# Two heads at a time in a prompt's attention, zero-padded score and latent operands, and another order at two joints

## The chip, the cores and the metric

The kernel runs on one core of one Trainium2 chip. The time is the device time of one execution in microseconds; of several runs the median is quoted. The engines are TensorE (PE in the profile, its weight loads PEld), VectorE (DVE), ScalarE (ACT), GpSimd (POOL) and SyncE (SP), which issues most transfers.

## The reference

Two layers of an encoder trunk run over 640 rows of 1024 channels: one prompt of 512 rows and eight streams of 16 new rows, each stream with 512 rows of past. A layer projects x to the inputs of three mixers and their gates, runs the mixers, merges them, and runs a squared-ReLU feed-forward, each of the two with a layer norm behind it. The mixer that matters here is latent attention with eight heads:

```
q_lat = einsum('bqhd,chd->bqhc', q_nope, w_uk)
s = einsum('bqhc,bkc->bhqk', q_lat, ckv) + einsum('bqhr,bkr->bhqk', q_rope, krope)
s = where(k_pos // 64 <= q_pos // 64, s * scale, -1e30)
p = softmax(s)
o_lat = einsum('bhqk,bkc->bqhc', p, ckv)
out = einsum('bqhc,chd->bqhd', o_lat, w_uv)
```

A head has 64 plain and 32 rotary dimensions, the latent has 256, values have 64. All is fp32.

## The kernel before, in words

Activations lie with channels on the partitions and the 640 rows along the free axis, in two halves of 320 (index i of names such as `x`, `r`, `P`). Most products are made exact to fp32 by three products in a rounded format: an operand is cut into a high and a low part (helper `split`, L378 on ScalarE and L379 on VectorE), and `mm3_steps` issues high x high (L437), low x high (L439) and high x low (L441). Other products are plain fp32 matmuls; the profile has two records for one of them, and one for a transpose. An order listing has one row for each instruction.

The prompt's attention is not absorbed: for each head `keys` and `queries` make 96-row operands, 64 plain rows and 32 rotary ones, cut in two (`kth`, `ktl`, `qh`, `ql`; three buffers of each). `heads_in(pr)` makes them for a pair of heads. The stage has 32 steps in a layer, one for each head h and block of 128 queries qt, in the order h = i // 4, qt = i % 4. Step i issues `score(i + 2)` (128 x up to 512 keys, three products), `value(i - 1)`, one piece of other work, `turn_p(i)` (transposes of the weights, tile `tp`, evicted to `pT`) and two more pieces. The softmax of a score goes over VectorE (mask, maximum), ScalarE (exponential with its sum) and VectorE (reciprocal, scaling). `value` multiplies into a tile `op` that holds a pair of heads: the even head in partitions 0 to 63, the odd one in 64 to 127. The pieces of other work are `heads_in` of the next pair, side projections (`mm_ca`, `mm_cg`, `mm_gc`, `mm_h`, three products each), and in the last eight steps `absorb`, which makes the streams' latent queries: `qlat` multiplies 64 rows of a head's `w_uk` by 64 rows of `qsn`, the streams' plain queries.

Behind it the streams run absorbed: `cut_keys(b)` cuts a stream's keys (`kT`, and for four streams together the rotary rows `kR`) into `kTh`, `kTl`, `kRh`, `kRl`; `rope_q(g)` lays the rotary queries of four streams into a tile with zeros elsewhere (`qzh`, `qzl`), and `score_s` (tile `ss`) multiplies three blocks, two of `kT` and one of `kR`, with three products each. Later `uv` turns the latent outputs into values, for two heads at a time.

Before the feed-forward stands a layer norm whose second half of rows is done under the first products of the first half: `plain(f, i)` makes the hidden block f for half i in 24 matmuls (tile `P`); `norm_starts` sums columns with ones (`pvn`), VectorE iterates the root (`rsyn`), `spread` broadcasts it (`rbn`), and `norm_cut` makes r and the cut x (`xh` on ScalarE, `xl` on VectorE, eight blocks). The first block of the second half needs all eight.

TensorE's instructions stand in the order in which the code issues them. On the other engines a scheduler sets the order by priorities; `first` raises that of the attention's own work, and `issue_after` holds an instruction behind a named one.

## Time and profile before

| | |
|---|---|
| median of 3 runs | 1978.42 us (1977.46 to 1981.24) |
| the profiled execution, its own time | 1979.2 us |
| its span | 1977.4 us |
| TensorE busy | 1953.8 us, 99% of the span |
| VectorE, ScalarE, GpSimd busy | 1349.3, 949.8 and 24.7 us |
| chain of work that ended last | 96% TensorE, 2% ScalarE, 1% VectorE |

The profile's times are those of the span, which begins with the first instruction and ends with the last; 1.8 us of the execution lie outside of it. A row of the timeline gives the start, the duration, engine, line, operation, output and inputs with partitions x elements, how many of them in a row, and in brackets the idle time ahead and what ended it. Matmuls overlap: a matmul's duration is longer than the time until the next may start, so the distance from start to start is what one costs. The line numbers are those of the kernel before.

### The profile page before, as it was taken

To read this page: it belongs to the slowest core of one execution; us is meant where nothing else is said; L and a number is where in the kernel's file an instruction comes from. 1 tells how busy PE (TensorE), PEld (TensorE's weight loads), DVE (VectorE), ACT (ScalarE), POOL (GpSimd) and SP (SyncE) were. 2 spreads that over 40 slices of the span, in tenths; PEclk is the share of its full clock that TensorE was granted. 3 is DMA by queue.
4 is the path that set the end of the run, shared out by engine and by line. 5 is a ranking of instruction groups with operands and counts; after the bars stand their busy time and mean duration, and the time that the engine had idled before them with its cause. 6 is when DMAs were issued, how large, how long until landed. Compare 5 with 4: busy or idle time off the path is not lost.

```text
span 1977.4 us, 33150 instructions
## 1 busy us (share of the span) xinstructions
PE 1953.8 (99%) x13264; PEld 1898.1 (96%) x13264; DVE 1349.3 (68%) x2936; ACT 949.8 (48%) x1880; POOL 24.7 (1%) x55
## 2 busy tenths in 40 slices
PE   9999999999999999999999999999999999999997
PEld 9887999999999999999997879999999999999997
DVE  5765669776586666776777556797755866667675
ACT  5564322244475545446556643323354665553473
POOL 0000000000000000000000000000000000000000
PEclk9999999999999999999999999999999999999998
DMA  6112322222222333213341134222232133332242
GB/s 204 52 36 92 131 81 82 77 66 85 65 75 83 121 128 118 86 65 107 108 155 57 36 96 148 66 82 65 75 90 62 58 107 122 114 107 86 64 129 75
DMA packets 59691, 180.62 MB, mean 91 GB/s; under 512 B 10384, under 2 KB 12832, under 8 KB 59536
## 3 DMA queue, kind: packets, MB, share of 16 engines
q1 hardware_dynamic: 57472, 172.01, 27.2%
q0 software_dynamic: 2064, 6.48, 1.1%
q8 instruction: 104, 1.70, 0.4%
q14 instruction: 51, 0.42, 0.1%
HBM read 173.78 MB, written 4.69 MB: 90 GB/s over the span
## 4 chain that ended last, share of the span: by engine, by line
PE 96%; ACT 2%; DVE 1%; DMA 0%; issue 0%; ACTq 0%; DVEq 0%
PE f L441 8%; PE f L439 8%; PE f L437 8%; PE mm_g L437 6%; PE mm_g L441 6%; PE mm_g L439 6%; PE op L817 2%; PE mix L437 2%; PE mix L439 2%; PE mix L441 2%; PE B L441 2%; PE C L437 2%; PE B L439 2%; PE C L441 2%; PE A L437 2%; PE C L439 2%
## 5 line engine op out<-in xcount | busy, mean ns | idle before, releaser
L226 ACT ACTIVATE wh<-raw 128x1024 fp32r<-128x1024 f32 (+3 forms) x170 | 166.7, 981 | 306.1 <-PE mm_g L439 201.2
L227 DVE TENSOR_TENSOR wl<-raw,wh 128x1024 fp32r<-128x1024 f32 (+3 forms) x170 | 191.4, 1126 | 129.6 <-ACT wh L226 126.2
L439 PE MATMUL f<-hl,wh 128*128 128x320 f32 x992 | 252.0, 309 | 0.0
L441 PE MATMUL f<-hh,wl 128*128 128x320 f32 x992 | 251.7, 309 | 0.0
L437 PE MATMUL f<-hh,wh 128*128 128x320 f32 x992 | 249.5, 309 | 0.0
L437 PE MATMUL mm_g<-xh,wh 128*128 128x320 f32 x768 | 181.9, 311 | 0.0
L441 PE MATMUL mm_g<-xh,wl 128*128 128x320 f32 x768 | 181.1, 309 | 0.0
L439 PE MATMUL mm_g<-xl,wh 128*128 128x320 f32 x768 | 180.4, 309 | 0.0
L439 PEld LDWEIGHTS f<-hl,wh 128*128 128x128 f32 x992 | 172.5, 188 | 0.0
L441 PEld LDWEIGHTS f<-hh,wl 128*128 128x128 f32 x992 | 172.3, 188 | 0.0
L437 PEld LDWEIGHTS f<-hh,wh 128*128 128x128 f32 x992 | 171.9, 188 | 0.0
L1077 DVE SCALAR_TENSOR_TENSOR cv<-U,vec,cv 128x320 f32<-128x320 f32 x360 | 134.4, 436 | 0.0
L437 PEld LDWEIGHTS mm_g<-xh,wh 128*128 128x128 f32 x768 | 129.8, 188 | 1.5 <-issue 0.3
L441 PEld LDWEIGHTS mm_g<-xh,wl 128*128 128x128 f32 x768 | 129.6, 188 | 0.2
L439 PEld LDWEIGHTS mm_g<-xl,wh 128*128 128x128 f32 x768 | 129.4, 188 | 0.0
L412 DVE TENSOR_TENSOR r<-r,f 128x320 f32<-128x320 f32 x192 | 85.4, 483 | 55.0 <-PE f L441 54.4
L226 ACT ACTIVATE wh<-sm 128x1024 fp32r<-128x1024 f32 x56 | 59.4, 1060 | 121.2 <-DVE sm L261 44.7
L227 DVE TENSOR_TENSOR wl<-sm,wh 128x1024 fp32r<-128x1024 f32 x56 | 68.5, 1223 | 49.9 <-PE C L441 28.6
L437 PE MATMUL mix<-mgh,wh 128*128 128x320 f32 x256 | 79.4, 311 | 0.0
L439 PE MATMUL mix<-mgl,wh 128*128 128x320 f32 x256 | 78.7, 309 | 0.0
L441 PE MATMUL mix<-mgh,wl 128*128 128x320 f32 x256 | 75.2, 309 | 0.0
L226 ACT ACTIVATE wh<-rx 128x1024 fp32r<-128x1024 f32 x28 | 29.7, 1060 | 89.2 <-PE f L439 76.9
(438 smaller groups left out, 5135.7 us busy)
## 6 DMA issues: line engine op xcount, KB each, us to landing
raw<-in_W_dram SPq DMA_DIRECT2D x204, 512.0 KB, 3.6
rx<-in_W_dram SPq DMA_DIRECT2D x28, 512.0 KB, 3.7
rxb<-in_W_dram SPq DMA_DIRECT2D x28, 512.0 KB, 3.7
kT<-in_ckvT_dram SPq DMA_DIRECT2D x16, 512.0 KB, 4.2
kM<-in_ckvM_dram SPq DMA_DIRECT2D x16, 512.0 KB, 4.0
raw<-in_W_dram SPq DMA_DIRECT2D x18, 384.0 KB, 3.1
raw<-in_W_dram SPq DMA_DIRECT2D x12, 256.0 KB, 2.7
x<-in_xT_dram SPq DMA_DIRECT2D x8, 320.0 KB, 6.1
```

Of the source, the lines that this page charges most:

```text
L226: nc.scalar.activation(out=wh[:, :n], in_=src, func=AF.Copy)
L227: nc.vector.tensor_tensor(out=wl[:, :n], in0=src, in1=R(wh[:, :n]), op=ALU.subtract)
L412: nc.vector.tensor_tensor(out=r[i][:, m, :], in0=r[i][:, m, :], in1=o, op=ALU.add)
L437: nc.tensor.matmul(o, wh, h[k], start=st, stop=False, skip_group_check=more)
L439: nc.tensor.matmul(o, wh, lo[k], start=False, stop=False, skip_group_check=more)
L441: nc.tensor.matmul(o, wl, h[k], start=False, stop=sp, skip_group_check=more)
L817: nc.tensor.matmul(op[r0:r0 + 64, qt * P:(qt + 1) * P], vt[kt // 2][:, kt % 2, h * 64:(h + 1) * 64], pT[:, kt * P:(kt + 1) * P], start=kt ...
L1077: nc.vector.scalar_tensor_tensor(out=o, in0=u, scalar=tap, in1=o, op0=ALU.mult, op1=ALU.add)
```

## The change

In the prompt's attention the steps now go through a pair of heads in the order of `PAIR`, both heads in turn. `value` does nothing for the even head and, with the odd one, issues the matmuls of both alternately, into the two column halves of the array. Key and query operands become 128-row tiles, three of each, whose rows 96 to 127 GpSimd fills with zeros once a layer. `qsn` gets 128 rows for every head, zeros in the half that belongs to the other head, and `qlat` multiplies all 128 rows. One gated tile buffer goes. `cut_keys` cuts the plain keys ahead of the rotary ones, and `rope_q` of the first streams is issued behind them. In the feed-forward, `pvn` and `rbn` are issued in the middle of a block's 24 matmuls, where they stood between blocks. The computed values are the same sums; the two layers are changed alike.

```diff
SIDE = (("ca", 0), ("cg", 0), ("ca", 1), ("cg", 1), ("gc", 0), ("h", 0), ("gc", 1), ("h", 1), ("gb", 0), ("gb", 1))
+PAIR = ((0, 0), (0, 1), (1, 0), (0, 2), (1, 1), (0, 3), (1, 2), (1, 3))
 KT2 = 2 * KT
...
     nc.vector.memset(one1, 1.0)
+    zero = cst.tile([P, 1], F32, name="zero")
+    nc.vector.memset(zero, 0.0)
     wu = psT.tile([P, 512], F32, tag="t", name="wu")
...
         qnl = pq.tile([P, 3, T], F32R, tag="qn", name="qnl", bufs=2)
-        qsn = pq.tile([P, 4, P], F32, tag="qsn", name="qsn", bufs=1)
+        qsn = pq.tile([P, 2, 4, P], F32, tag="qsn", name="qsn", bufs=1)
+        nc.gpsimd.memset(qsn, 0.0)
         vt = [pq.tile([P, 2, 512], F32, tag="kM", name=f"vt{i}", bufs=2) for i in range(2)]
...
             if n != "h" and n != "gb":
-                t = held[n] = pf.tile([P, T], F32, tag="g2" if n == "cg" else "g1", name=f"{n}s{l}{c}", bufs=1 if n == "cg" else 2)
+                t = held[n] = pf.tile([P, T], F32, tag="g2" if n == "cg" else "g1", name=f"{n}s{l}{c}", bufs=1)
             for i, a, b in HALVES:
...
         pp = pp_stk.enter_context(pool(f"pp{l}", side="right"))
-        kth = [pp.tile([96, SEQ], F32R, name=f"kth{i}") for i in range(3)]
-        ktl = [pp.tile([96, SEQ], F32R, name=f"ktl{i}") for i in range(3)]
+        kth, ktl, qth, qtl = ([pp.tile([P, SEQ], F32R, name=f"{n}{i}") for i in range(3)] for n in ("kth", "ktl", "qth", "qtl"))
+        for i in range(3):
+            for t in (kth[i], qth[i], ktl[i], qtl[i]):
+                nc.gpsimd.tensor_copy(t[96:P, :], zero[96:P, 0:1].to_broadcast([32, SEQ]))
         def key_rope(i):
...
             for e in range(2):
-                qk.append((pp.tile([96, SEQ], F32R, tag="qh", name=f"qh{l}_{pr}_{e}", bufs=3), pp.tile([96, SEQ], F32R, tag="ql", name=f"ql{l}_{pr}_{e}", bufs=3)))
+                qk.append((qth[(2 * pr + e) % 3], qtl[(2 * pr + e) % 3]))
             @first
             def queries(i, c0, c1, o):
...
                 if i:
-                    nc.scalar.activation(out=qsn[:, pr, :], in_=o[:, SEQ - HF:], func=AF.Copy, scale=SCALE)
+                    for e in range(2):
+                        nc.scalar.activation(out=qsn[64 * e:64 * e + 64, e, pr, :], in_=o[64 * e:64 * e + 64, SEQ - HF:], func=AF.Copy, scale=SCALE)
             @first
             def keys(ko):
...
                 yield
+        def at_step(i):
+            e, qt = PAIR[i % 8]
+            return 2 * (i // 8) + e, qt
         @first
         def score(i):
-            h, qt = divmod(i, 4)
+            h, qt = at_step(i)
             qh, ql, kh, kl = qt_h[h]
...
         def turn_p(i):
-            h, qt = divmod(i, 4)
+            h, qt = at_step(i)
             n, pb = P * (qt + 1), mid.pop(i)
...
             nc.scalar.activation(out=pT[:, :n], in_=tp[:, :n], func=AF.Copy)
-            pv[i] = pT
+            pv[h, qt] = pT
         @first
         def value(i):
-            h, qt = divmod(i, 4)
-            pT, pr, r0 = pv.pop(i), h // 2, 64 * (h % 2)
-            if i % 8 == 0:
+            h, qt = at_step(i)
+            if h % 2 == 0:
+                return
+            pr = h // 2
+            if qt == 0:
                 pv["o"] = mm_tile(f"op{l}_{pr}", 512, "op")
             op = pv["o"]
+            pTs = [pv.pop((2 * pr + e, qt)) for e in range(2)]
             for kt in range(qt + 1):
-                nc.tensor.matmul(op[r0:r0 + 64, qt * P:(qt + 1) * P], vt[kt // 2][:, kt % 2, h * 64:(h + 1) * 64], pT[:, kt * P:(kt + 1) * P], start=kt == 0, stop=kt == qt)
-            if i % 8 == 7 and pr < 3:
+                for e in range(2):
+                    hd = 2 * pr + e
+                    nc.tensor.matmul(op[64 * e:64 * e + 64, qt * P:(qt + 1) * P], vt[kt // 2][:, kt % 2, hd * 64:(hd + 1) * 64], pTs[e][:, kt * P:(kt + 1) * P], start=kt == 0, stop=kt == qt)
+            if qt == 3 and pr < 3:
                 nc.scalar.activation(out=oT[:, pr, :SEQ], in_=op, func=AF.Copy)
...
             for ct in range(2):
-                os = [mm_tile(f"qlat{l}{ct}{e}", 512) for e in range(2)]
-                for pr in range(4):
-                    for e, o in enumerate(os):
-                        nc.tensor.matmul(o[:, pr * P:(pr + 1) * P], wukT[64 * e:64 * e + 64, pr, ct * P:(ct + 1) * P], qsn[64 * e:64 * e + 64, pr, :], start=True, stop=True)
+                for e in range(2):
+                    o = mm_tile(f"qlat{l}{ct}{e}", 512)
+                    for pr in range(4):
+                        nc.tensor.matmul(o[:, pr * P:(pr + 1) * P], wukT[:, pr, ct * P:(ct + 1) * P], qsn[:, e, pr, :], start=True, stop=True)
                         if pr == 3:
...
             def cut_keys(b):
...
                 kt_s[b] = [ps.tile([P, 2, NK], F32R, tag=f"kT{n}", name=f"kT{n}{l}{b}", bufs=2) for n in "hl"]
+                nc.vector.tensor_copy(kT[:, :, PAST:], ckv[:, :, SEQ + b * NQ:SEQ + (b + 1) * NQ])
+                ins = split(*kt_s[b], kT)
                 if kR is not None:
...
                         nc.vector.tensor_copy(kR[rg, PAST:], krope[rg, SEQ + (b + j) * NQ:SEQ + (b + j + 1) * NQ])
-                nc.vector.tensor_copy(kT[:, :, PAST:], ckv[:, :, SEQ + b * NQ:SEQ + (b + 1) * NQ])
-                ins = split(*kt_s[b], kT)
-                if kR is not None:
                     split(*kr_s[b // 4], kR)
...
                 nc.gpsimd.memset(t, 0.0)
-            for z in qz:
-                nc.scalar.activation(out=z, in_=cnew.rearrange("p b (j q) -> p (b j) q", j=2), func=AF.Copy)
-            @first
-            def rope_q(g):
-                for j in range(4):
-                    rg = slice(DR * j, DR * j + DR)
-                    split(qz[0][rg, j, :], qz[1][rg, j, :], qsr[rg, g].rearrange("p h q -> p (h q)"))
+            def rope_q(g, after=(None, None)):
+                for n in range(2):
+                    with tc.issue_after(after[n].ins) if after[n] else ExitStack():
+                        if g == 0:
+                            nc.scalar.activation(out=qz[n], in_=cnew.rearrange("p b (j q) -> p (b j) q", j=2), func=AF.Copy)
+                        for j in range(4):
+                            rg = slice(DR * j, DR * j + DR)
+                            src, dh = qsr[rg, g].rearrange("p h q -> p (h q)"), qz[0][rg, j, :]
+                            if n == 0:
+                                nc.scalar.activation(out=dh, in_=src, func=AF.Copy)
+                            else:
+                                nc.vector.tensor_tensor(out=qz[1][rg, j, :], in0=src, in1=R(dh), op=ALU.subtract)
             olat = pq.tile([P, 2, NH, NB, NQ], F32, tag="qr", name=f"olat{l}", bufs=1)
...
                 nc.scalar.activation(out=oT[:, 3, :SEQ], in_=pv["o"], func=AF.Copy)
-            rope_q(0)
+            first(rope_q)(0, (i_h, i_l))
             with tc.issue_after(i_l.ins):
...
                     cut_keys(4)
-                    rope_q(1)
+                    first(rope_q)(1)
                 if b % 2 and b < NB - 1:
...
             x_blk = {}
-            def plain(f, i):
+            def plain(f, i, between=None):
                 if i == 0:
                     x_blk[f] = W.next(l, ("ff1", 0, f), hold=True)
-                o = bank(f"P{l}_{f}_{i}")
-                prod(o, [x_blk[f]("ff1", k, f) for k in range(KT)], xs_of((i,))[0])
+                o, ret = bank(f"P{l}_{f}_{i}"), None
+                for k, _ in enumerate(mm3_steps([o], [x_blk[f]("ff1", k, f) for k in range(KT)], xs_of((i,)))):
+                    if k == 3 and between:
+                        ret = between()
                 if i:
...
                 hidden(f, i, work(f"h{f}_{i}"), o)
+                return ret
             X = chunk(7)
             plain(X[0], 0)
-            spread = ahead(norm_starts, 1, ss1[1], ntp)
-            plain(X[1], 0)
-            rb1 = ahead(spread)
+            spread = plain(X[1], 0, lambda: ahead(norm_starts, 1, ss1[1], ntp))
+            rb1 = plain(X[2], 0, lambda: ahead(spread))
             ahead(norm_cut, 1, rb1)
-            plain(X[2], 0)
             plain(X[3], 0)
```

TensorE, layer 0, the first values of the first pair of heads (tile `op`; around them scores `s`, a side projection `mm_ca`, the next pair's queries `uqn` and transposes `tp`). Before:

```order
L437 MATMUL s_0_3_1075<-kth_909,qh_0_0_939 128x512
L439 MATMUL s_0_3_1075<-ktl_912,qh_0_0_939 128x512
L441 MATMUL s_0_3_1075<-kth_909,ql_0_0_940 128x512
L817 MATMUL op_0_1086<-pT_0_0_1065,vt_209 64x128
L437 MATMUL mm_ca_1_1_1071<-xh_100,wh_842 128x320
L439 MATMUL mm_ca_1_1_1071<-xl_102,wh_842 128x320
L441 MATMUL mm_ca_1_1_1071<-xh_100,wl_843 128x320
L804 MATMUL tp_0_1_1091<-ident,p_0_1_1039 128x128 x2
```

and after:

```order
L441 MATMUL s_0_3_1153<-kth_912,qth_918 128x512
L443 MATMUL s_0_3_1153<-ktl_915,qth_918 128x512
L445 MATMUL s_0_3_1153<-kth_912,qtl_921 128x512
L837 MATMUL op_0_1164<-pT_0_0_1083,vt_212 64x128
L837 MATMUL op_0_1164<-pT_1_0_1141,vt_212 64x128
L441 MATMUL uqn_1_1_1167<-qnh,wh_954 128x320
L443 MATMUL uqn_1_1_1167<-qnl,wh_954 128x320
L445 MATMUL uqn_1_1_1167<-qnh,wl_955 128x320
L818 MATMUL tp_0_2_1171<-ident,p_0_2_1100 128x128 x3
```

The value matmul of head 1's first block (`pT_1_0`) has moved up to head 0's; in longer groups the two heads alternate for two, three and four blocks in the same way.

TensorE, layer 0, a step of the last pair, with the two `qlat` of the step (their operands are `qsn` and the weights `wukT`). Before:

```order
L437 MATMUL s_6_3_1858<-kth_909,qh_3_0_1645 128x512
L439 MATMUL s_6_3_1858<-ktl_912,qh_3_0_1645 128x512
L441 MATMUL s_6_3_1858<-kth_909,ql_3_0_1646 128x512
L817 MATMUL op_3_1869<-pT_6_0_1852,vt_209 64x128
L835 MATMUL qlat_1847<-qsn,wukT_1761 128x128
L804 MATMUL tp_6_1_1872<-ident,p_6_1_1799 128x128 x2
L835 MATMUL qlat_1848<-qsn,wukT_1761 128x128
L437 MATMUL mm_h_0_0_1812<-xh_99,wh_1527 128x320
```

and after:

```order
L441 MATMUL s_6_3_1910<-kth_912,qth_918 128x512
L443 MATMUL s_6_3_1910<-ktl_915,qth_918 128x512
L445 MATMUL s_6_3_1910<-kth_912,qtl_921 128x512
L837 MATMUL op_3_1921<-pT_6_0_1860,vt_212 64x128
L837 MATMUL op_3_1921<-pT_7_0_1904,vt_212 64x128
L854 MATMUL qlat_1900<-qsn,wukT_1765 128x128
L818 MATMUL tp_6_2_1925<-ident,p_6_2_1873 128x128 x3
L854 MATMUL qlat_1900<-qsn,wukT_1765 128x128
L441 MATMUL mm_h_0_0_1817<-xh_101,wh_1532 128x320
```

The two `qlat` of a step still stand on both sides of the transposes, but now belong to one head and one output tile, and half of the steps have no values.

VectorE, layer 0, behind the broadcast root of the second half's norm (`t` are pieces of a combination for a later stage, `hl` and `T1l` low parts of hidden blocks and of that combination). Before:

```order
L1168 SCALAR_TENSOR_TENSOR r_4551<-r_4551,vec,rbn_6024 128x320 x8
L1182 TENSOR_TENSOR t_00_6119<-r_4551,r_4550 128x320
L379 TENSOR_TENSOR hl_15_0_6019<-h_00_6017,hh_15_0_6018 128x320
L1182 TENSOR_TENSOR t_01_6123<-r_4551,r_4550 128x320
L1152 SCALAR_TENSOR_TENSOR xl_102<-r_4551,vec,xh_100 128x320
L1182 TENSOR_TENSOR t_02_6127<-r_4551,r_4550 128x320
L1152 SCALAR_TENSOR_TENSOR xl_102<-r_4551,vec,xh_100 128x320
L1182 TENSOR_TENSOR t_03_6131<-r_4551,r_4550 128x320
L1152 SCALAR_TENSOR_TENSOR xl_102<-r_4551,vec,xh_100 128x320 x4
L1186 SCALAR_TENSOR_TENSOR t_00_6135<-r_4551,vec,t_00_6119 128x320
L1152 SCALAR_TENSOR_TENSOR xl_102<-r_4551,vec,xh_100 128x320 x2
```

and after, from the first `xl` on:

```order
L1175 SCALAR_TENSOR_TENSOR xl_104<-r_4560,vec,xh_102 128x320
L1205 TENSOR_TENSOR t_02_6136<-r_4560,r_4559 128x320
L1175 SCALAR_TENSOR_TENSOR xl_104<-r_4560,vec,xh_102 128x320
L1205 TENSOR_TENSOR t_03_6140<-r_4560,r_4559 128x320
L1175 SCALAR_TENSOR_TENSOR xl_104<-r_4560,vec,xh_102 128x320 x3
L1209 SCALAR_TENSOR_TENSOR t_00_6144<-r_4560,vec,t_00_6128 128x320
L1175 SCALAR_TENSOR_TENSOR xl_104<-r_4560,vec,xh_102 128x320
L1209 SCALAR_TENSOR_TENSOR t_01_6148<-r_4560,vec,t_01_6132 128x320
L1175 SCALAR_TENSOR_TENSOR xl_104<-r_4560,vec,xh_102 128x320
L383 TENSOR_TENSOR hl_30_0_6064<-h_00_6062,hh_30_0_6063 128x320
L1209 SCALAR_TENSOR_TENSOR t_02_6152<-r_4560,vec,t_02_6136 128x320
L1175 SCALAR_TENSOR_TENSOR xl_104<-r_4560,vec,xh_102 128x320
```

Two more combination pieces and a low part of another hidden block have moved ahead of the last `xl`.

## Rows read from the trace of the kernel before

**Rows 1.** The page's busy times: us, share of the span, instructions.

```profile
PE 1953.8 (99%) x13264; PEld 1898.1 (96%) x13264; DVE 1349.3 (68%) x2936; ACT 949.8 (48%) x1880; POOL 24.7 (1%) x55
```

**Rows 2.** TensorE's waits: who waited for whom, us, times, longest.

```profile
PE ss L439 <- DVE kTl L379: 5.0, 2, 2.5
...
PE pvn L462 <- DVE s L417: 2.4, 2, 1.4
```

**Rows 3.** Stretches of layer 0's attention: busy us of each engine, clock, DMA.

```profile
123.40:147.60 24.20, 24.20 (x153) 19.89 (x152) 15.13 (x44) 15.28 (x39) 1.45 (x2) 1.00 0.11 28
160.00:186.50 26.50, 26.50 (x156) 19.77 (x155) 11.33 (x35) 13.17 (x33) 0.84 (x3) 1.00 0.16 52
```

**Rows 4.** TensorE's timeline around two groups of values: start, us, operation.

```profile
92.50 0.28 PE L439 MATMUL s<-ktl,qh 96*128 96x256 f32 x1
92.62 0.28 PE L441 MATMUL s<-kth,ql 96*128 96x256 f32 x1
92.83 0.65 PE L817 MATMUL op<-pT,vt 128*64 128x128 f32 x4
93.41 0.41 PE L437 MATMUL uqn<-qnh,wh 128*128 128x320 f32 x1
93.66 0.31 PE L439 MATMUL uqn<-qnl,wh 128*128 128x320 f32 x1
93.81 0.31 PE L441 MATMUL uqn<-qnh,wl 128*128 128x320 f32 x1
...
95.62 0.87 PE L817 MATMUL op<-pT,vt 128*64 128x128 f32 x6
```

**Rows 5.** TensorE's timeline at the streams' value projection in layer 0.

```profile
269.84 1.97 PE L1024 MATMUL uv<-olat,wuv 128*64 128x128 f32 x32
271.74 0.41 PE L437 MATMUL mm_g<-xh,wh 128*128 128x320 f32 x1
```

**Rows 6.** Groups of instructions by line and shape: count, busy us, mean ns, idle before.

```profile
L817 PE MATMUL op<-pT,vt 128*64 128x128 f32 x320 | 48.6, 283 | 0.0
```

**Rows 7.** TensorE's timeline in a step with latent queries, layer 0.

```profile
165.40 0.28 PE L441 MATMUL s<-kth,ql 96*128 96x256 f32 x1
...
166.19 0.49 PE L835 MATMUL qlat<-qsn,wukT 64*128 64x128 f32 x2
166.61 0.55 PE L804 MATMUL tp<-ident,p 128*128 128x128 f32 x3
167.09 0.48 PE L835 MATMUL qlat<-qsn,wukT 64*128 64x128 f32 x2
...
167.75 0.31 PE L439 MATMUL mm_h<-xl,wh 128*128 128x320 f32 x1
```

**Rows 8.** GpSimd's timeline ahead of layer 0's attention.

```profile
77.29 0.92 POOL L607 DMA_DIRECT2D out_conf_dram<-U  x1
```

**Rows 9.** Groups of instructions by line and shape, on GpSimd.

```profile
L919 POOL MEMSET wz<- 128x512 f32 x2 | 1.1, 529 | 62.2 <-PE qlat L835 62.2
```

**Rows 10.** TensorE's timeline at the first score of layer 0.

```profile
84.14 0.34 PE L437 MATMUL s<-kth,qh 96*128 96x256 f32 x1
```

**Rows 11.** VectorE's timeline: the softmax of layer 0's last score.

```profile
175.62 0.69 DVE L791 TENSOR_REDUCE st<-s 128x1 f32<-128x512 f32 x1
...
177.91 0.48 DVE L795 TENSOR_SCALAR p<-p,st 128x512 f32<-128x512 f32 x1
```

**Rows 12.** VectorE's timeline at the first stream's keys, layer 0.

```profile
186.90 1.22 DVE L379 TENSOR_TENSOR qzl<-qsr,qzh 32x128 fp32r<-32x128 f32 x4
188.15 1.26 DVE L379 TENSOR_TENSOR kTl<-kT,kTh 128x1056 fp32r<-128x1056 f32 x1
...
189.93 0.69 DVE L379 TENSOR_TENSOR kRl<-kR,kRh 128x528 fp32r<-128x528 f32 x1
```

**Rows 13.** VectorE's timeline at the last cut of x, layer 0's feed-forward.

```profile
570.31 1.01 DVE L1152 SCALAR_TENSOR_TENSOR xl<-r,vec,xh 128x320 fp32r<-128x320 f32 x2
```

**Rows 14.** TensorE's timeline at the product that reads it.

```profile
571.51 0.31 PE L439 MATMUL P<-xl,wh 128*128 128x320 f32 x1
```

## The prediction

> **What bounds the kernel now.** Read the share of the engines first: TensorE's matmul row is busy for 99% of the span, the other engines for 68% or less [rows 1]. So only two things can move the time: matmul work that gets shorter, and a wait of TensorE that goes or comes. Second, read the list of TensorE's waits: it is short, and the largest ones that this change touches are 5.0 us before the first stream's scores (two times, one per layer) and 2.4 us before the column sums `pvn` [rows 2]. All else is hidden as long as it stays hidden. Third, read how close the matmuls stand to each other in time; a busy row says nothing of that, since a matmul counts as busy while it waits in the array for its neighbour. The window of the attention stage gives the reserve of the other engines: 24.2 us of eight steps hold 15.1 us of VectorE and 15.3 of ScalarE, and the last eight steps, 26.5 us, hold 11.3 and 13.2 [rows 3].
>
> **Value matmuls: switches and rate.** In a row of plain matmuls of 320 columns one starts 0.15 us after the other (93.66 to 93.81), and a score of 256 columns 0.12 us after the one before [rows 4]. Around a group of value matmuls (64 output columns of the array) it is different: from the last score to the second matmul behind the group are 1.04 us (92.62 to 93.66), where the score's 0.12, two value matmuls at 0.22 and one matmul at 0.15 make 0.71 [rows 4]. That one value matmul costs 0.22 follows from the durations of the groups: 0.65 us with four records, 0.87 with six, and two records are one fp32 matmul [rows 4]. So each group pays about 0.34 us for going to 64 columns and back.
>
> The trace has a precedent for what the change makes of the values. The streams' value projection `uv` does the same arithmetic, 64 columns, fp32, two heads in turn on the two column halves of one output tile: its 32 records (16 matmuls) start at 269.84 and the next matmul at 271.74 [rows 5]. Those 1.90 us, less 0.14 of entering that the prompt's group shows too (0.58 less 0.44), are 0.11 us for a matmul, half of 0.22. The two column halves run beside each other when their matmuls alternate, and not when one head's stand together, as in `op` now: 48.6 us for 320 records [rows 6], 0.152 us each. The new order alternates the heads exactly as `uv` does. There are 160 `op` matmuls in both layers, so the halving is worth 160 x 0.11 = 17.6 us.
>
> The even head's group disappears into the odd one's: 32 groups in a layer become 16. Of them 24 stand in the first 24 steps and become 12, which saves 12 x 0.34 = 4.1 us a layer.
>
> **Latent queries in the last eight steps.** There a step runs score, values, half a latent-query matmul pair, a transpose, the other half, a projection. From the last score (165.40) to the second projection matmul (167.75) are 2.35 us [rows 7]. At full-array rates the pieces would be 0.12 for the score, 0.44 for two values, 0.22 for each of two `qlat`, 0.33 for three transposes of one record, and 0.15: 1.48. The excess, 0.87 us, is paid at each of eight steps: 7.0 a layer. With 128 rows of zeros and queries the `qlat` matmuls have the shape of the transposes and projections around them, and a step without values pays nothing; the four steps that keep a group pay 0.09 ahead of it, 0.14 in it and some 0.06 behind: 0.29. That leaves 1.2 a layer, so 5.8 are saved. With the 4.1 above it is 9.9 a layer, 19.8 in both.
>
> The latent queries are also where the rows and a rule part. They show a `qlat` 0.42 us long from its start to the next start (166.19 to 166.61), and a transpose between it and its fellow on the other half of the rows [rows 7]: nothing overlaps. The Trainium skill ("TensorE: Matmul & The Clock Gate", the section on why this matters for kernels) says against such padding that matmuls with few rows should stay sliced so that each lands in its own row group, where they run concurrently. By it the padding would give up one of every two matmuls, 16 x 0.22 = 3.5 us in all, and the sum would end 3.5 us higher, near 1949; the trace disagrees here, since the order never puts the two halves next to each other.
>
> **Score operands padded to 128 rows.** The scores of 96 rows already start 0.12 us apart for 256 columns, which is the 0.15 of 320 columns in proportion [rows 4]; there is nothing to gain, and the row count doesn't lengthen a matmul: 0. The zeros are written by GpSimd, twelve copies of 32 x 512 a layer behind its output transfer, which ends at 78.2 in layer 0 (77.29 + 0.92) [rows 8]. No such copy is in the trace; the nearest row is its fill of 128 x 512, 0.53 us [rows 9], so I take 0.55. The first score at 84.1 [rows 10] needs four of them (80.4), the second head's, two short steps later at some 87.6, eight (82.6). Hidden; for the price from which it isn't, see the rivals. The fill of the padded queries, twice the size and so 1.1 us, stands at the layer's start, where GpSimd has only loads for much later behind it. One buffer in place of two for the gated tiles is hidden as well, since VectorE has read one before the projection of the next ends; a late read would hold one eviction, by at most the piece of 0.5 us that reads it.
>
> **First score.** ScalarE now runs the second head's query piece, 0.33 us at 83.20 in its timeline, ahead of the keys that the first score waits for, and the latent queries in two pieces. TensorE waits there already, so it is added: about 0.3 us in layer 0 and 0.1 in layer 1, +0.4.
>
> **Softmax under a shorter stage.** Eight steps shrink from 24.2 us by 20 x 0.11 + 4 x 0.34 = 3.6, to 20.6; the last eight from 26.5 by 2.2 + 5.8 = 8.0, to 18.5. VectorE and ScalarE are then 61 to 74% busy, so neither is a bound by sum; by latency it is closer. A row's maximum starts at 175.62 and its normalised weights end at 178.39 [rows 11]; with the mask ahead of it that is some 3 us. TensorE asks for them two steps later: 5.2 us in a mean pair of steps, 4.6 in the last eight, near 4 for two short ones. ScalarE also has key pieces in between, which a pair of heads now brings close together. Waits of 0 to 4 us a layer are possible; I take 1.5, since the mean slack is over 1 us and only the short steps and the change of a pair use it up: +3 in all.
>
> **First stream.** TensorE waits for the low part of the first keys, which VectorE begins at 188.15 behind 1.22 us of rotary-query pieces [rows 12]. Now the keys come first, so their low part ends near 188.2 in place of 189.4. But the third block of the same score needs the rotary keys' low part (now 189.93 + 0.69 [rows 12], then about 189.5) and the queries' pieces behind it, so most of the wait only moves a block further; the raw rotary keys still load into the queries' buffer behind the last `qlat`, as before. Bounds from these rows: 2.5 gained a layer (the whole wait), or 0.6 lost; I take 0.5 gained: -1.0.
>
> **Feed-forward start.** `pvn` moves twelve matmuls (1.8 us) later, so its waits, 1.06 us in layer 0 and 1.36 in layer 1 (2.4 [rows 2]), go. But the broadcast behind it also comes later by what the wait doesn't cover, about 0.5 us, and VectorE then has to make r and the eight low parts xl. Before, the last two xl start at 570.31 and end at 571.32 [rows 13], and the matmul that reads the last one starts at 571.51 [rows 14]: 0.2 us of slack. In the new order two more combination pieces stand among the xl's at about 0.46 us each, and the one `hl` in the stretch is exchanged for another; the last xl ends near 572.7. TensorE waits there instead, and ends some 1.2 us later in layer 0 and 0.8 in layer 1: +2.0. If the scheduler's order leaves the xl's in time it is -2.4; at most +2.5.
>
> **The sum.** -17.6 - 19.8 + 0.4 + 3.0 - 1.0 + 2.0 = -33.0 us. Against the profiled run of 1979.2 (span 1977.4 and 1.8 around it) that is 1946.2; the median of the runs is 0.8 lower, so **1945**. With no softmax wait and the better ends of the last two terms it is -37.4 + 0.4 - 5.0 - 2.4 = -44, near 1934; with the worse ends, 8 us of softmax, +1.2 and +2.5, it is -25, 1953.
>
> **Rivals.** (A) The heads' matmuls do not run beside each other in `op`, and only switches are saved: -19.8 + 4.4 = -15.4, near 1963. For it speaks that `op` alternates within an accumulation over key blocks, two groups of one bank open together, while in `uv` each is short; against it that `uv` also accumulates over two blocks in one bank at the full rate. 10%.
>
> (B) The softmax sets the pace: every one of the 64 steps of both layers waits 0.13 to 0.25 us more than I took, 8 to 16 us back, 1953 to 1961. For it: three wide rows stand at the end of each pair, and a pair's keys, queries and exponentials meet on ScalarE; against it: a quarter of both engines' time stays idle. 13%.
>
> (C) Slower: the zero fills on GpSimd are far dearer than its fill row, since these write a quarter of the rows as rounded fp32 from a broadcast value. Eight are needed within 87.6 - 78.2 = 9.4 us. They cancel a gain of 16.5 us a layer when eight take 9.4 + 16.5 = 25.9 us, 3.2 us each, six times the row; above it the kernel is slower, at 4 us each by 2 x 6.1 = 12 us: 1990. 3%.
>
> (D) The change doesn't do what it says: waits on the odd head hold back every gain, or the alternation is undone, and the time stays at 1978. 2%.
>
> **How the numbers follow.** The forecast has 72%. The range from 1935 to 1960 holds it and nearly all of B, and leaves out A, C, D and a little on each side: under 2 in 10. A difference under 0.2% (4 us) can't be told from none. Faster by more than that: forecast, A and B, 0.94; within it 0.03 (D, and a mixture of waits); slower 0.03 (C).
>
> **What would show it.** After: `op` with about 24 us busy in place of 48.6, as `uv` per record; a `qlat` 0.22 us from the next start; 16 groups of values in a layer; the stage's eight steps near 20.6 and 18.5 us; TensorE's waits with a new entry at the P products for xl and none at `pvn` in mid-kernel; the wait for the first stream's scores at about 2 us a layer. Wrong are: `op` unchanged per record (A), waits of transposes for the normalised weights or of values for pT above 4 us a layer (B), scores waiting for GpSimd (C).

## The result, and the profile after

| | before | after |
|---|---|---|
| median | 1977.94 us (4 runs) | 1947.4 us (4 runs, 1945.57 to 1947.79) |
| profiled span | 1977.4 us | 1945.7 us |

The ratio is 0.9841 (95% interval 0.9824 to 0.9859). Faster, as forecast, with the time 2.4 us above the forecast and inside its range. By the medians the change is worth 30.5 us, by the two profiled spans 31.7.

The busy times and TensorE's waits (us in total, times, longest) of the changed kernel answer to [rows 1, 2]:

```profile
PE 1920.1 (99%) x13264; PEld 1878.9 (97%) x13264; DVE 1353.1 (70%) x2937; ACT 948.6 (49%) x1888; POOL 45.9 (2%) x81
```

```profile
PE s L441 <- DVE ktl L383: 2.7, 1, 2.7
PE ol L1003 <- ACT wz L990: 2.6, 1, 2.6
PE rbn L485 <- DVE rsyn L479: 2.5, 1, 2.5
PE ss L443 <- DVE kTl L383: 2.5, 2, 1.3
PE P L443 <- DVE xl L1175: 2.3, 7, 0.6
PE pvn L466 <- DVE s L1405: 1.8, 1, 1.8
...
PE ss L443 <- DVE kRl L383: 0.6, 2, 0.3
PE ol L1004 <- DVE spN L993: 0.6, 1, 0.6
```

TensorE lost 34 us of busy time and is still busy for 99%. In the list the wait for `kTl` has halved, the `pvn` wait in mid-kernel is gone (the 1.8 us that are left stand at the kernel's end, as before), and two entries are new: the P products wait for `xl`, as forecast, and the first latent outputs (`ol`) wait 2.6 us in layer 1, which no step of the prediction has. The list has no waits of transposes or value matmuls, which a slow softmax would show.

The groups by line and shape, answering to [rows 6]:

```profile
L837 PE MATMUL op<-pT,vt 128*64 128x128 f32 x320 | 25.4, 283 | 0.1
L854 PE MATMUL qlat<-qsn,wukT 128*128 128x128 f32 x64 | 12.9, 287 | 0.0
```

and TensorE's timeline in two steps of layer 0, one with values and one with latent queries and no values (to set beside [rows 4, 7]):

```profile
107.94 0.28 PE L443 MATMUL s<-ktl,qth 128*128 128x256 f32 x1
108.05 0.28 PE L445 MATMUL s<-kth,qtl 128*128 128x256 f32 x1
108.26 1.09 PE L837 MATMUL op<-pT,vt 128*64 128x128 f32 x16
109.29 0.41 PE L441 MATMUL mm_cg<-xh,wh 128*128 128x320 f32 x1
109.54 0.31 PE L443 MATMUL mm_cg<-xl,wh 128*128 128x320 f32 x1
...
157.40 0.34 PE L445 MATMUL s<-kth,qtl 128*128 128x384 f32 x1
157.57 0.38 PE L854 MATMUL qlat<-qsn,wukT 128*128 128x128 f32 x2
157.79 0.38 PE L818 MATMUL tp<-ident,p 128*128 128x128 f32 x2
158.01 0.39 PE L854 MATMUL qlat<-qsn,wukT 128*128 128x128 f32 x2
158.15 0.39 PE L441 MATMUL mm_h<-xh,wh 128*128 128x320 f32 x1
```

Eight value matmuls take 1.03 us from start to the next start, 0.14 of entering and 0.11 each, the rate of `uv`. The entering and leaving is unchanged: 0.21 from the last score, 0.25 to the second matmul behind. A `qlat` without values beside it costs 0.22, and nothing around it costs more than at the full rate. `op` fell from 48.6 to 25.4 us.

The next table cuts every profiled run at the same first starts of TensorE's tiles, so that what happens at the very start of the kernel doesn't blur it; us, layer 0 / layer 1. "v to s" is from the first value projection to the first score, "s to ss" the prompt's attention, "ss to uv" the streams' attention, "P to f" the start of the feed-forward. The names in the first column are the experiments below.

| | v to s | s to ss | ss to uv | P to f |
|---|---|---|---|---|
| before | 12.14 / 14.23 | 102.44 / 103.07 | 83.26 / 83.21 | 30.86 / 31.17 |
| after | 12.62 / 14.93 | 84.46 / 84.92 | 81.49 / 85.04 | 32.23 / 32.24 |
| f1, after again | 12.62 / 14.92 | 84.49 / 83.38 | 82.02 / 85.04 | 32.25 / 32.24 |
| f2, pairs alone | 12.14 / 14.25 | 89.36 / 90.03 | 83.34 / 83.04 | 30.49 / 31.00 |
| e1, heads in turn | 12.62 / 14.93 | 87.28 / 86.20 | 82.11 / 85.12 | 32.23 / 32.24 |
| e2, qlat 64 rows | 12.61 / 14.95 | 89.07 / 89.31 | 82.01 / 83.45 | 32.24 / 32.23 |
| e9, scores 96 rows | 12.32 / 14.47 | 85.11 / 85.75 | 80.97 / 81.57 | 32.24 / 32.23 |
| e4, keys first alone | 12.14 / 14.23 | 102.40 / 103.08 | 85.13 / 82.14 | 30.94 / 30.74 |
| e4b, queries first | 12.61 / 14.92 | 84.75 / 85.20 | 82.48 / 83.28 | 32.24 / 32.23 |
| e3, sums between | 12.61 / 14.92 | 84.47 / 84.90 | 82.22 / 82.03 | 30.58 / 30.66 |
| e7, weights later | 12.61 / 14.92 | 84.49 / 83.38 | 82.03 / 82.09 | 32.23 / 32.25 |
| f3, e3 and e7 | 12.61 / 14.92 | 84.48 / 83.38 | 80.52 / 82.07 | 30.94 / 30.91 |
| f4, e3 and e9 | 12.33 / 14.49 | 85.12 / 84.22 | 81.35 / 82.67 | 30.48 / 30.87 |
| e10, e3, e7 and e9 | 12.33 / 14.46 | 85.11 / 85.76 | 81.48 / 79.97 | 30.60 / 32.83 |

From before to after: +1.2 ahead of the first scores, -36.1 in the prompt's attention, +0.1 in the streams' (one layer 1.8 less, the other 1.8 more), +2.4 in the feed-forward's start. With +0.7 of small rest that is the -31.7 of the spans.

The granted clock has to be read beside this table. In some stages it falls for a few microseconds behind a wait of TensorE. Of the four stages of attention (the prompt's and the streams', in two layers) it fell in three in the kernel before (the prompt's in layer 1, the streams' in both layers), in two in the changed kernel (both in layer 1), and in f1, the same kernel again, in the streams' of both layers. So the -1.8 of the streams' layer 0 sets a stage with a low clock against one without: f1, which has it as the kernel before, is 1.2 us shorter there. The prompt's layer 1 of the kernel before, in two stretches of 4 us from its first score (the length and TensorE's busy time stand first, its granted clock is the third number from the end):

```profile
1064.54:1068.54 4.00, 4.00 (x20) 4.00 (x21) 1.31 (x7) 1.02 (x4) 0.00 (x0) 0.70 0.00 0
1068.54:1072.54 4.00, 4.00 (x23) 3.39 (x22) 1.91 (x7) 1.28 (x4) 0.00 (x0) 0.87 0.00 0
```

The changed kernel's and f1's are shown in the last section.

### The profile page after: what moved, and what is told of

It is laid out like the page before. It is cut to its first block, busy times and chain, and to the rows that moved or that the text cites. A ratio compares the mean times of both kernels' runs of the same rounds, so it can differ in the third digit from the quotient of the medians.

```text
span 1945.7 us, 33206 instructions
## 1 busy us (share of the span) xinstructions
PE 1920.1 (99%) x13264; PEld 1878.9 (97%) x13264; DVE 1353.1 (70%) x2937; ACT 948.6 (49%) x1888; POOL 45.9 (2%) x81
```

## Experiments

**The pairs alone (f2).** The kernel before with the new order of steps and the new `value`, nothing else:

```diff
+            e, qt = PAIR[i % 8]
+            return 2 * (i // 8) + e, qt
...
-            h, qt = divmod(i, 4)
+            h, qt = at_step(i)
...
+            if h % 2 == 0:
+                return
```

> The kernel before with the pairs' order and the alternating values alone: no zeros, latent queries on 64 rows, old orders at both joints. By the terms: 160 x 0.11 = 17.6, 24 groups of the first 24 steps less in both layers 8.2, and four of the last eight steps without a group 0.14 each, 1.1: -27, about 1951, and from the first score to the first stream's scores 13.4 us less in each layer (from 102.4 to 89.0). The rival: a good part of the attention's gain hangs on the zero padding (the array switching for 96 rows too), and less than 10 us a layer come.

Measured: 1951.75 us, ratio 0.9868 (0.9854 to 0.9881). The prompt's attention takes 13.1 and 13.0 us less, where 13.4 were expected, and no softmax wait came. In layer 1 both runs have the low clock. The pairing alone is worth 26 us of the 31, and it hangs on no padding.

**Alternation or grouping (e1).** The changed kernel with the loops of `value` exchanged:

```diff
-            for kt in range(qt + 1):
-                for e in range(2):
+            for e in range(2):
+                for kt in range(qt + 1):
```

> The changed kernel, but inside a group of values all matmuls of the even head stand ahead of those of the odd one. Groups, switches and all else stay. If the alternation gives the column halves their overlap, 160 matmuls cost 0.22 us in place of 0.11: +17.6 us, about 1965, and op is busy for about 48 us again. The rival, that the gain comes from fewer and longer groups, expects no difference: 1947, op busy for 25 us.

Measured: 1952.08 us, ratio 0.9869 (0.9854 to 0.9883): neither. From the first score to the first stream's scores it is 2.8 us a layer longer (layer 1 against f1, since neither has a low clock there), 5.6 in all, where 17.6 were expected for the first theory and 0 for the rival. The profile shows why, in its groups and in the timeline of groups of eight, twelve and sixteen records, to be set beside 1.09 for sixteen above:

```profile
L837 PE MATMUL op<-pT,vt 128*64 128x128 f32 x320 | 31.0, 283 | 0.0
```

```profile
100.57 0.66 PE L837 MATMUL op<-pT,vt 128*64 128x128 f32 x8
...
105.47 1.14 PE L837 MATMUL op<-pT,vt 128*64 128x128 f32 x12
...
108.86 1.58 PE L837 MATMUL op<-pT,vt 128*64 128x128 f32 x16
```

A group with two blocks (eight records) takes 0.66 us with the heads in turn, as much as alternated. Longer groups overlap in part only: 1.14 and 1.58 where alternated groups took 0.88 and 1.09. The starts of the single records of the last group say how: eight of them follow each other from 108.86 to 109.68, mostly 0.11 us apart, and eight more from 109.36 to 110.17, so the second head's first record started when three of the first head's eight had yet to start. (The records don't name the head; two chains, each as far apart as one head's records were before, are how the starts read.) The groups of eight and twelve show the same three records. So here TensorE started matmuls of the free column half ahead of three records that stand before them in its order; what the change did first of all was to put the two heads into one group, and the alternation adds 5.6 us to that.

**Latent queries on 64 rows (e2).** The operands are sliced again, all else as changed:

```diff
-                        nc.tensor.matmul(o[:, pr * P:(pr + 1) * P], wukT[:, pr, ct * P:(ct + 1) * P], qsn[:, e, pr, :], start=True, stop=True)
+                        nc.tensor.matmul(o[:, pr * P:(pr + 1) * P], wukT[64 * e:64 * e + 64, pr, ct * P:(ct + 1) * P], qsn[64 * e:64 * e + 64, e, pr, :], start=True, stop=True)
```

> The changed kernel, with the latent queries multiplied on 64 rows again (in the new order of heads; the zero rows are not read). By the excess read from the step of before, four steps of a layer with values pay 0.87 in place of 0.29 us and four without pay 0.73 in place of 0: +5.2 a layer, +10.5 in all, about 1958, and a qlat stands 0.4 us from its follower. The rival from the rule on row groups (Trainium skill, TensorE: Matmul & The Clock Gate): halves on different rows overlap, so 64 rows are no slower or up to 3.5 us faster: 1944 to 1947.

Measured: 1955.65 us, ratio 0.9886 (0.9872 to 0.9901), 8.2 us slower than the change. The prompt's attention is 4.6 us a layer longer in layer 0 and 4.4 in layer 1, near the 5.2; `qlat` is busy for 15.5 us again, as before, where the changed kernel has 12.9:

```profile
L854 PE MATMUL qlat<-qsn,wukT 64*128 64x128 f32 x64 | 15.5, 322 | 0.0
```

So the padding is worth some 9 us in this order. The rule on row groups from the page "TensorE: Matmul & The Clock Gate" of the Trainium skill (its section on why this matters for kernels) is about matmuls that land in distinct row groups, which then run concurrently. No run here has two such matmuls next to each other: in the kernel before a transpose stands between the two halves [rows 7], and in e2 the two `qlat` of a step belong to one head and use the same half. Whether two halves side by side would cost less than the padding is not tested. What the Trainium skill's "TensorEngine Tiling (Array Packing)" says under its key properties, that a change of the tiling mode drains the engine, agrees with the 0.87 us that a step loses around such matmuls [rows 7].

**Scores of 96 rows (e9).** Three fixed buffers of 96 rows, no fills:

```diff
-        kth, ktl, qth, qtl = ([pp.tile([P, SEQ], F32R, name=f"{n}{i}") for i in range(3)] for n in ("kth", "ktl", "qth", "qtl"))
-        for i in range(3):
-            for t in (kth[i], qth[i], ktl[i], qtl[i]):
-                nc.gpsimd.tensor_copy(t[96:P, :], zero[96:P, 0:1].to_broadcast([32, SEQ]))
+        kth, ktl, qth, qtl = ([pp.tile([96, SEQ], F32R, name=f"{n}{i}") for i in range(3)] for n in ("kth", "ktl", "qth", "qtl"))
```

> The changed kernel with score operands of 96 rows in three fixed buffers, no zero fills. If the padding does nothing for the matmuls but the fills slow VectorE ahead of the first score (its 32 x 512 pieces take 1.09 us beside them, 0.68 without), the first score comes 0.5 us earlier in layer 0 and 0.7 in layer 1: -1.2, about 1946. The rival, that 96 rows make the array switch between scores and their neighbours as 64 do: 64 scores with 0.2 to 0.3 us each, +13 to +19, 1960 to 1966.

Measured: 1943.98 us, ratio 0.9826 (0.9812 to 0.9839). The first score comes 0.30 and 0.46 us earlier. The attention then is 0.6 us longer in layer 0 and 0.8 in layer 1; in layer 0, 0.55 of that is a wait of the first stream's scores' very first matmul that their next wait gives back (0.7 in place of 1.3 us). The scores themselves cost the same (their median records take 340, 333 and 334 ns, padded 336, 333 and 335), so the rival falls. The rest of the 3 us is the missing `ol` wait in layer 1, which other edits move as well (below). The fills themselves are told of in the last section.

**The sums of the norm (e3).** `pvn` and `rbn` between blocks again:

```diff
-            spread = plain(X[1], 0, lambda: ahead(norm_starts, 1, ss1[1], ntp))
-            rb1 = plain(X[2], 0, lambda: ahead(spread))
+            spread = ahead(norm_starts, 1, ss1[1], ntp)
+            plain(X[1], 0)
+            rb1 = ahead(spread)
             ahead(norm_cut, 1, rb1)
+            plain(X[2], 0)
```

> The changed kernel with the column sums and the broadcast of the second half's norm between blocks again. Predicted term, and the trace: the waits of the P products for xl go, those of the sums for s (1.06 and 1.36 us) come back; from the first P to the first f 1.4 us less in layer 0 and 1.1 in layer 1: -2.4, about 1945. The rival, that the later sums are a gain by themselves and the xl waits come from the shorter stage ahead: no change or slower, 1947 to 1950.

Measured: 1941.07 us, ratio 0.9812 (0.9799 to 0.9826). P to f is 1.65 and 1.58 us shorter, the waits for `xl` are gone, and the sums wait 1.6 us for both layers:

```profile
PE pvn L466 <- DVE s L1407: 1.8, 1, 1.8
PE pvn L466 <- DVE s L421: 1.6, 2, 0.8
```

So 3.2 us of the gain are this edit's own. The other 3.0 lie in the streams' attention of layer 1, where nothing was edited.

**The first stream's keys (e4, e4b).** The new order of `cut_keys` and `rope_q` put alone into the kernel before (e4), and taken alone from the changed one (e4b):

```diff
...
-            rope_q(0)
+            first(rope_q)(0, (i_h, i_l))
...
```

> The kernel before, with the order of the first stream's keys alone changed. The theory from the two traces: the wait of 2.5 us a layer becomes 1.3 and 0.3, and the granted clock, which stood at 0.62 to 0.86 for some microseconds behind the long wait, stays at 1.00, worth another 1.7 us a layer: -2.7 a layer, -5 in all, about 1973. The rival, as predicted: only part of the wait is gained and the clock costs nothing of note: -1 in all, 1977.

> The changed kernel with the old order of the first stream's keys and rotary queries. Layer 0 loses the 1.0 us of wait and 1.7 us of clock: +2.7. In layer 1 TensorE then comes later to the first latent outputs, where it now waits 2.6 us for weights' transfers through ScalarE, so that wait and the low clock behind it shrink: by the theory that the two waits trade, layer 1 gains 0 to 1.6, and the sum is about +1 to +3: 1949. The rival, that they are independent, expects +2.7 in both: 1953.

Measured: e4 1977.92 us, ratio 0.9999 (0.9990 to 1.0009); e4b 1947.72, ratio 0.9844 (0.9830 to 0.9859). Neither moved the time. (The profiled execution of e4 is the longest of its ten, 1980.4 us of 1976.7 to 1980.4, so what follows need not hold for the median.) In e4 the wait for `kTl` fell from 2.5 to 1.3 us in both layers, yet layer 0's streams took 1.9 us longer and layer 1's 1.1 less. e4b against the changed kernel: +1.0 and -1.8, where the theory that the waits trade had +2.7 and 0 to -1.6. (Layer 0 of e4b has the low clock; against f1, which has it too, it is +0.5.) In e4's profiled execution, what the shorter first wait gains in layer 0 is lost again later, and the windows show how. In layer 0 (four stretches of 4 us from the first stream's scores) the clock stayed up for 12 us, and TensorE then waited 2.7 us at a side projection:

```profile
187.74:191.74 4.00, 2.44 (x18) 2.02 (x16) 3.93 (x11) 2.54 (x6) 1.34 (x2) 1.00 0.85 284
191.74:195.74 4.00, 4.00 (x30) 4.00 (x30) 3.60 (x9) 2.07 (x4) 0.00 (x0) 1.00 0.36 111
195.74:199.74 4.00, 2.29 (x19) 2.08 (x17) 1.16 (x4) 0.44 (x1) 0.00 (x0) 1.00 1.02 381
199.74:203.74 4.00, 3.01 (x12) 2.97 (x13) 3.29 (x5) 3.01 (x6) 0.00 (x0) 0.63 0.17 65
```

What it waited for is in TensorE's waits and in ScalarE's timeline there:

```profile
PE mm_gc L437 <- ACT gcs L592: 2.7, 1, 2.7
```

```profile
199.30 1.06 ACT L226 ACTIVATE wh<-raw 128x1024 fp32r<-128x1024 f32 x1 [3.62 <-DMA raw<-in_W_dram]
200.26 0.42 ACT L592 ACTIVATE gcs<-mm_gc 128x320 f32<-128x320 f32 x1
```

ScalarE stood 3.6 us before the cut of a block of weights, whose transfer had not landed, and the eviction of the side projection's bank was queued behind it. In layer 1 of the same run the granted clock was 0.91 and 0.66 in the first two stretches, TensorE came some 1.5 us later to the same place, and it did not wait there: that layer keeps its 1.1 us.

**One block of weights later (e7).** In the changed kernel the 2.6 us of `ol` have the same source: ScalarE's timeline in layer 1, and TensorE's wait:

```profile
1145.19 1.06 ACT L228 ACTIVATE wh<-raw 128x1024 fp32r<-128x1024 f32 x1 [4.08 <-DMA raw<-in_W_dram]
1146.15 1.07 ACT L382 ACTIVATE kTh<-kT 128x1056 fp32r<-128x1056 f32 x1
...
1148.16 0.70 ACT L978 ACTIVATE sp<-ss,sst 128x528 f32<-128x528 f32 x1 [0.60 <-DVE sst L977]
...
1148.85 0.59 ACT L990 ACTIVATE wz<-stp 128x512 f32<-128x512 f32 x1
```

```profile
1149.49 0.71 PE L1003 MATMUL ol<-wz,kM 128*128 128x128 f32 x4 [2.59 <-ACT wz L990]
```

The edit keeps the loader from fetching that block until the first latent outputs are issued (`ahead_w` is how many blocks of weights it may run ahead, 2 before):

```diff
             cut_keys(1)
+            W.ahead_w = 1
...
                 value_s(b)
+                if b == 0:
+                    W.ahead_w = 2
+                    W._ahead()
```

> The changed kernel with the load and cut of one block of weights moved behind the first stream's latent outputs, from ahead of them. If ScalarE, standing at that cut until its transfer lands, is what holds the first latent outputs in layer 1, that wait of 2.6 us and some 1.7 us of low clock behind it go: -4 in layer 1, -0.6 in layer 0: about 1943. The rival: the transfers as a whole are late, and the wait moves to the keys or to the block's own products: 1946 to 1948.

Measured: 1942.48 us, ratio 0.9817 (0.9804 to 0.9831). The streams' attention of layer 1 is 3.0 us shorter and the `ol` waits are gone in both layers; layer 0 is 0.5 us longer, by a low clock of its own behind the first wait. The wait did not move to another place. Other edits that touch no weights remove the wait of layer 1 too (below), so what ties it to the transfer is ScalarE's timeline above rather than e7 alone.

**The changed kernel again (f1), and combinations (e10, f3, f4).** f1 is the changed kernel without an edit; the others combine the edits of e3, e7 and e9.

> The changed kernel once more, on the chip of the three others. If its wait of 2.6 us for the first latent outputs in layer 1 belongs to the kernel, it is there again and the time is 1947, and the single edits undone are worth what they showed against it; if it belongs to one run or chip, the time is 1943 to 1944 and only some 2 us of what they showed is theirs.

> The changed kernel with the three edits together: sums between blocks, scores of 96 rows without fills, one block of weights later. If each does what its own run expects and they don't meet: -2.4 - 1.2 - 4.6 = -8, about 1939.

> The changed kernel with the sums between blocks and one block of weights later, scores padded as in the change. If the two add up against the changed kernel: -3.2 for the sums (1.6 a layer as their run's trace shows) and -2 to -4 for the weights: 1940 to 1942. If the wait in layer 1 isn't the kernel's own, only the sums: -3.

> The changed kernel with the sums between blocks and scores of 96 rows without fills, weights where they were. Against the changed kernel -3.2 for the sums and, by the traces from the start of the layer to the first stream's scores, between -0.5 and +0.5 for the missing fills, with a shorter wait of that stream's scores (0.7 in place of 1.3): -4 to -6, 1941 to 1943.

Measured: f1 1946.83 us (ratio 0.9838, 0.9825 to 0.9852), and the 2.6 us of `ol` in layer 1 are there again, so they are the kernel's own. f3 1942.42 (0.9819, 0.9806 to 0.9832), f4 1942.32 (0.9821, 0.9808 to 0.9834), e10 1940.33 (0.9809, 0.9796 to 0.9822) with all three edits. The single gains don't add: 6.3, 3.4 and 4.9 us less than the change, 14.6 together, and 7.1 with all three. Most of the reason is in the column of the streams' attention: each of the three edits, and e4b too, takes the same 1.8 to 3.5 us from layer 1. Once the `ol` wait is gone, only the 1.6 us a layer of e3 are left for certain; in e10 even these are blurred in layer 1, where the sums waited 1.5 us and the clock fell. In f4 the wait has moved, to the side projection as in e4:

```profile
PE mm_gc L441 <- ACT gcs L598: 2.4, 1, 2.4
```

All of e3, e7, e9, e10, f3 and f4 have lower medians than the changed kernel in its two runs. e10 has the lowest; the intervals of the six overlap one another, and only e10's lies clear of both of the changed kernel's.

## Why the prediction was right, point by point

**Value matmuls: right in size, too strict in its reason.** The rate of 0.11 us came out to the digit (the price of a group is 0.33 by its own rows, 1.04 less 0.71, and not 0.34), and with the 12 groups fewer the prompt's attention without the padding lost 26.1 us in both layers (f2), where the terms gave 26.9. The step "not when one head's stand together" was wrong as a general sentence: [rows 6] showed heads whose groups stood a step apart. With both heads in one group they overlap in part even in turn (e1); the alternation is 5.6 us of the 17.6. Rival A is excluded by `op` itself.

**Latent queries: right in kind, somewhat too large.** 5.8 us a layer were forecast for the last eight steps, 5.2 of them the padding's by the same terms; measured are 4.6 and 4.4 (e2). A `qlat` that follows values directly still costs 0.33 us to the next start in place of 0.22 (160.04 to 160.37 in TensorE's timeline), 0.05 more than the term allowed for, four times a layer.

**Padded scores: right, 0.** The scores cost the same with 96 rows (e9).

**First score: too small.** Forecast +0.4, measured +0.48 and +0.70, 1.2. The missing part is what the zero fills do to VectorE, which the prediction took as hidden; e9 gives 0.30 and 0.46 of it back.

**Softmax: too dear.** Taken at 3 us, it cost nothing that the list of waits shows. The prompt's attention lost 36.1 us, against 37.4 forecast before the softmax; in layer 1 both kernels have the low clock, so the comparison is fair, and the other terms were 1.3 too large, 0.8 of it in the pairs (f2). (f1 has no low clock there and is 1.5 us shorter, 83.38 and not 84.92; set against the kernel before, which has it, that would pass for gain.) Rival B is excluded. So is C: the fills took at most 1.07 us each, a third of its price, and no score waits for GpSimd.

**First stream: wrong.** Forecast -1.0, measured +0.1, and with f1, whose clock falls in the same two layers as before, +0.6. The first wait fell from 2.5 to 1.3 us a layer and the third block waits 0.3 us for `kRl`, so 0.9 us a layer went there, within the bounds; but that the wait's end moves the stage's end was the step that failed. In layer 1 the 2.6 us of `ol` came in its place, 1.8 us more in all. A weights' transfer that ScalarE stands before decides when the first latent outputs and the side projection's bank come (e4, e7), and TensorE that arrives sooner waits there. The prediction read the stage's first wait and not the queue behind it.

**Feed-forward: right in kind and size.** Forecast +1.2 and +0.8, measured +1.37 and +1.07: the sums' wait went, and the P products wait 2.3 us for `xl`. VectorE's timeline shows the two additional combination pieces and the low part `hl` among the last `xl`:

```profile
551.19 0.54 DVE L1209 SCALAR_TENSOR_TENSOR t<-r,vec,t 128x320 f32<-128x320 f32 x1
551.65 0.54 DVE L1175 SCALAR_TENSOR_TENSOR xl<-r,vec,xh 128x320 fp32r<-128x320 f32 x1
552.12 0.48 DVE L383 TENSOR_TENSOR hl<-h,hh 128x320 fp32r<-128x320 f32 x1
552.52 0.54 DVE L1209 SCALAR_TENSOR_TENSOR t<-r,vec,t 128x320 f32<-128x320 f32 x1
552.98 0.54 DVE L1175 SCALAR_TENSOR_TENSOR xl<-r,vec,xh 128x320 fp32r<-128x320 f32 x1
```

The last one ends at 553.5, counted from the first P product 1.4 us behind its old place, as forecast; in the two layers TensorE has seven waits for them. Undone, it is worth 3.2 us (e3) and not 2.4, since the sums wait only 0.8 us a layer there, where they waited 1.06 and 1.36 before.

So the sum of -33.0 met -31.7 with errors that cancel: the softmax was 3.0 us too dear, against 1.3 of the attention's other terms, 1.1 at the streams, 0.8 at the first scores, 0.4 in the feed-forward and 0.7 of rest. There is luck in it too: the profiled run of before had one low clock more than those of the changed kernel, some 1.5 us (an estimate from the changed kernel's and f1's 84.92 and 83.38), which no term forecast.

## What to carry to other kernels

Two heads with 64 output columns belong into one group on the two column halves of one tile (26 us here), and operands of 64 rows that stand between full matmuls were cheaper with zeros, some 9 us for 32 matmuls here; read both prices as distances from start to start around one group, and look for a tile in the same trace that already does it. Where a stage becomes shorter, follow the transfers that are issued inside it: ScalarE, standing 3.6 and 4.1 us before a late one, held all that was queued behind it. And cut the trace at fixed tiles, with the granted clock of each stage beside it, before adding up the gains of single edits, since several may remove the same wait.

## What the runs showed of the hardware that was not expected

**GpSimd and VectorE slow each other.** The zero fills took 1.07 us each while VectorE cut the rotary keys, and 0.62 from 83.8 on, beside other work of VectorE or none; VectorE's three cuts took 3.12 us beside them, and 1.89 in e9, which has no fills:

```profile
79.80 1.07 POOL L728 CAST ktl<-zero 32x512 fp32r<-32x512 f32 x1
...
83.83 0.62 POOL L728 CAST ktl<-zero 32x512 fp32r<-32x512 f32 x1
```

```profile
79.30 3.12 DVE L383 TENSOR_TENSOR ktl<-krope,kth 32x512 fp32r<-32x512 f32 x3
...
83.33 1.14 DVE L763 SCALAR_TENSOR_TENSOR qtl<-uqn,qth 64x192 fp32r<-64x192 f32 x3
```

```profile
80.24 1.89 DVE L383 TENSOR_TENSOR ktl<-krope,kth 32x512 fp32r<-32x512 f32 x3
```

The Trainium skill's "GPSIMD Engine Reference" says in its specifications that GpSimd shares memory interfaces with VectorE and contends with its instructions that have two inputs in SBUF, as these cuts do; the trace agrees, with 0.68 against 1.09 us for a cut. The fill at 83.83 ran beside the pieces of L763, one of whose inputs is `uqn`, an output tile of TensorE, and took 0.62.

**A wait of 1.3 to 2.7 us may be followed by a low clock, or not.** The changed kernel and f1 have the same wait ahead of layer 1's first score (2.7 and 2.6 us). Their windows from there on, the changed kernel's first, f1's second:

```profile
1047.00:1051.00 4.00, 3.41 (x16) 3.44 (x17) 1.59 (x7) 0.62 (x3) 1.00 (x2) 0.67 0.00 0
1051.00:1055.00 4.00, 4.00 (x27) 3.99 (x27) 2.04 (x8) 1.38 (x7) 0.00 (x0) 0.90 0.00 0
```

```profile
1048.40:1052.40 4.00, 3.44 (x26) 3.46 (x26) 1.85 (x9) 1.02 (x4) 0.95 (x2) 1.00 0.00 0
1052.40:1056.40 4.00, 4.00 (x30) 3.99 (x29) 2.50 (x11) 1.90 (x7) 0.00 (x0) 1.00 0.01 4
```

The granted clock was 0.67 and 0.90 in the one, a mean of the levels of 1.2 and 2.4 GHz, and 1.00 in the other, and the stage took 1.54 us more in the first. The same difference stands between several pairs of runs in the streams' attention. In all profiled runs each of the table's last three columns, in each layer, either keeps its clock or has falls that take 1.5 to 1.7 us in all (each stretch's length times the share of the clock that is missing in it). So from a single profile a gain of 1.5 us in a stage can't be told from a low clock that happened to be there or not.

**The same transfer takes 4.6 or 6.1 us.** ScalarE could start the cut of the weights' block 6.1 us behind the transfer's issue in layer 1 of the changed kernel (1139.11 to 1145.19), and 4.6 in layer 0 (175.86 to 180.41). All four runs with the long `ol` wait in layer 1 (the changed kernel, f1, e1, e2) have the 6.1 to 6.2 us there. In e3, which has no such wait, the transfer is issued at the same place, 6.6 us behind the stream's first score, and takes 4.6. So the issue is not what moved; why the transfer itself takes longer, and why edits elsewhere change that, stays open.
